# A two-layer hybrid decoder trunk on one core: the key blocks' and compressed keys' transposes and the pool branch's product stand later in TensorE's order

## The chip, the core and the metric

The kernel runs on one core of a Trainium2 chip. The core has five engines, each with its own instruction stream that it works off in order: TensorE (PE in the profile, its weight loads PEld) for matrix products, VectorE (DVE), ScalarE (ACT), GpSimd (POOL) and SyncE (SP), which here only issues DMAs. An instruction that has to wait for another engine waits at the head of its own stream, and all that is behind it waits too. The metric is the device time of one execution in microseconds (us), lower is better. It is given as the median of several runs.

## What is computed

The reference is a trunk of two layers on 512 tokens of width 1024, in float32:

```python
def _hybrid_layer(x, c, ...):
    mod = (jax.nn.silu(c) @ ada_w + ada_b).reshape(B, N_MOD, D_MODEL)
    x = x + 0.5 * g1 * _swiglu(_modulate(_rms_norm(x, norm_ffn1), sh1, sc1), ffn1_w_in, ffn1_w_out)
    h = _modulate(_rms_norm(x, norm_mix), sh2, sc2)
    u_pool, u_q, u_kv, u_gate, u_s5 = jnp.split(h @ w_in, IN_OFFSETS, axis=-1)
    y_pool = _rms_norm(_pool_mixer(u_pool, pool_w, pool_b, pool_scale), n_pool)
    y_nsa = _rms_norm(_nsa_mixer(u_q, u_kv, u_gate, ...), n_nsa)
    y_s5 = _rms_norm(_s5_mixer(u_s5, ...), n_s5)
    x = x + g2 * (jnp.concatenate([y_pool, y_nsa, y_s5], axis=-1) @ w_out)
    x = x + 0.5 * g3 * _swiglu(_modulate(_rms_norm(x, norm_ffn2), sh3, sc3), ffn2_w_in, ffn2_w_out)
    return x
```

The change lies in the middle step, the mixer. Three branches read the same projected input. The pool branch takes differences of windowed means and multiplies them by a small matrix per group. The NSA branch is attention with 8 query heads on 2 key heads: it needs keys and values of the tokens (normalised, rotated), keys and values compressed over 32 tokens by a small network, and the queries. The S5 branch is a linear recurrence.

## The kernel before

Every large product is made of three matrix products of 128x128 blocks whose operands are split into a high and a low part (`mm3`); the parts are made by ACT (high) and DVE or POOL (low). TensorE's work is the bulk of the time; DVE, ACT and POOL evacuate PSUM, normalise, split and scan.

**What sets the order.** The kernel is written as Python generators (one per chain of work), and a small planner (`Sched`, lines 337 to 378) steps them at build time. Each operation adds a cost to its engine's planned time, and a generator that says `yield t` is resumed when the planned time has come to `t`. An instruction enters its engine's stream when its generator is resumed. So `yield t + 1500.0` means: what comes next in this chain is put into the stream 1500 planned ns later than its inputs are planned to be ready, and other chains' instructions go ahead of it. The planned times set nothing but the order of the streams; on the chip each instruction waits for its own inputs. The planner's costs on TensorE are 233 ns for a matmul of 512 columns with split operands, 117 ns for 256 columns, 110 ns for a transpose, 222 ns for an unsplit one of up to 128 columns.

**PSUM and temporaries.** There are 8 PSUM banks and 9 temporary buffers of 128x512. A chain takes them at planned times (`wbank`, `bank`, `tmpn`, the last one first come, first served) and puts them back; a bank that is taken again carries a true wait on the chip for whoever read it last.

**The mixer's order on TensorE**, as the streams of both layers have it:
1. keys and values for the compression and the tokens' keys, one half of the tokens after the other (L1931 to 1966); each half ends with two blocks of keys that go through `qk_chain` with kind "k" (L1646);
2. the S5 projection (L1986 to 1994), and among its first matmuls the 16 transposes of the first half's two key blocks (L1694, four sets of four: high and low part of each block);
3. `compress(0)`, the compressed keys' first product, 16 unsplit matmuls (L1583), and among them the 16 transposes of the second half's two key blocks;
4. the pool projection, 48 matmuls (L2009); after its first nine come the S5 drive products (`s5_half`, L1751), one group for each of two halves of the channels, real parts first; three matmuls further on the compressed keys' second product (L1596);
5. `compress(1)` for the values, then their projection, 96 matmuls in four blocks (L2017); after 18 of them the two transposes of the compressed keys (L1637, 1638), after 30 more the pool branch's product of the first channel half (L1912), and after 12 more the S5 output products (L1802 to 1804), first half and second half;
6. the S5 branch's transposes and gate (L1831, L1843), the second pool product, both branches' norms (`norm_apply`), mixed with the query projection (L2270 to 2279), then attention mixed with the first half of the output projection.

**The chains that the change touches.** `qk_chain` for keys: ACT squares, DVE sums, POOL takes the power -0.5, DVE scales, POOL multiplies by gains and rotates, ACT makes the high part (L1685, 1686), DVE the low part (L1688), TensorE transposes, ACT (high) or DVE (low) evacuates (L1699). It holds two temporaries until its transposes. `compress_post` (L1591): a gelu on ACT, the second product, for the keys a norm and a rotation, then the two transposes; it holds a PSUM bank and two temporaries. `pool_chain` (L1885): sums over windows on POOL, a last step on DVE (L1909), the product, its evacuation, then the same for the second channel half, then the norm; it holds four temporaries from start to end. `s5_evac` (L1967) copies the S5 projection out of PSUM, 16 copies on ACT and 16 on DVE; `s5_chain` starts the drive products 3000 planned ns after them.

## Time and profile before

| | us |
|---|---|
| median of 3 runs | 2024.93 (2024.28 to 2029.98) |
| the profiled execution, whole time | 2025.7 |
| the profiled execution, span of the trace | 2023.9 |
| busy time of TensorE in the span | 1939.0 (96%) |
| of VectorE | 1601.9 (79%) |
| of ScalarE | 910.6 |
| of GpSimd | 530.6 |

Between the span and the whole time of the profiled execution lie 1.8 us. The page of the profile gives the busy time of each engine; the timeline gives an engine's instructions in order of time, like ones in a row merged into one row, and in square brackets how long the engine was idle before it and which engine and line ended that; the view by windows gives each engine's busy time and the granted TensorE clock (1.00 is 2.4 GHz, 0.50 is 1.2 GHz) in chosen stretches. `x4` counts instructions; an unsplit f32 matmul counts as two. Line numbers are those of helpers: L507 is every matmul, L523 every transpose, L458 every ACT operation, L467 and L471 DVE's with two and three operands, L494 POOL's.

### The profile page before, as it was taken

To read this page: it belongs to the slowest core of one execution; us is meant where nothing else is said; L and a number is where in the kernel's file an instruction comes from. 1 tells how busy PE (TensorE), PEld (TensorE's weight loads), DVE (VectorE), ACT (ScalarE), POOL (GpSimd) and SP (SyncE) were. 2 spreads that over 40 slices of the span, in tenths; PEclk is the share of its full clock that TensorE was granted. 3 is DMA by queue.
4 is the path that set the end of the run, shared out by engine and by line. 5 is a ranking of instruction groups with operands and counts; after the bars stand their busy time and mean duration, and the time that the engine had idled before them with its cause. 6 is when DMAs were issued, how large, how long until landed. Compare 5 with 4: busy or idle time off the path is not lost. (4 is left out here: it accounts for less than half of the span.)

```text
span 2023.9 us, 32544 instructions
## 1 busy us (share of the span) xinstructions
PE 1939.0 (96%) x12586; PEld 1740.2 (86%) x12586; DVE 1601.9 (79%) x2806; ACT 910.6 (45%) x1652; POOL 530.6 (26%) x755
## 2 busy tenths in 40 slices
PE   5999999998998899999999999999999989999999
PEld 3788888897887898999989899999888788898989
DVE  7789877487777788989779797788878779686866
ACT  3422222243666553534455353534437655453533
POOL 6049201744444400000020200065546360000000
PEclk9999999998998899999999999999999999999999
DMA  8668777231201125555122231413211012313222
GB/s 306 231 229 290 281 260 275 100 114 55 70 25 43 62 85 197 177 199 185 64 106 93 96 132 67 146 43 135 86 44 53 21 43 72 126 64 125 96 103 74
DMA packets 71147, 251.66 MB, mean 124 GB/s; under 512 B 8016, under 2 KB 10448, under 8 KB 70480
## 3 DMA queue, kind: packets, MB, share of 16 engines
q1 hardware_dynamic: 70992, 249.58, 35.0%
q8 instruction: 99, 1.62, 0.3%
q14 instruction: 56, 0.46, 0.1%
HBM read 247.45 MB, written 2.10 MB: 123 GB/s over the span
## 5 line engine op out<-in xcount | busy, mean ns | idle before, releaser
L507 PE MATMUL p<-s,s 128*128 128x256 f32 (+3 forms) x11926 | 1885.4, 319 | 64.9 <-DVE s L471 24.6
L507 PEld LDWEIGHTS p<-s,s 128*128 128x128 f32 x11926 | 1664.6, 191 | 249.4 <-DVE s L467 31.8
L458 ACT ACTIVATE s<-s 128x1024 fp32r<-128x1024 f32 (+6 forms) x910 | 623.1, 714 | 782.2 <-PE p L507 424.0
L467 DVE TENSOR_TENSOR s<-s,s 128x1024 fp32r<-128x1024 f32 (+9 forms) x868 | 758.5, 901 | 220.7 <-ACT s L458 214.5
L494 POOL TENSOR_TENSOR s<-s,s 128x256 f32<-128x256 f32 (+11 forms) x335 | 272.8, 833 | 251.0 <-DVE s L478 99.4
L494 POOL TENSOR_TENSOR s<-s 128x8 f32<-128x8 f32 (+4 forms) x224 | 155.2, 698 | 533.0 <-ACT s L458 362.5
L458 ACT ACTIVATE s<-p 128x512 f32<-128x512 f32 (+10 forms) x381 | 184.8, 502 | 224.7 <-PE p L507 160.3
L467 DVE TENSOR_TENSOR s<-p,s 128x512 f32<-128x512 f32 (+8 forms) x325 | 192.9, 605 | 55.0 <-ACT s L458 34.8
L471 DVE SCALAR_TENSOR_TENSOR s<-s,s 128x1024 f32<-128x1024 f32 (+3 forms) x179 | 197.9, 1110 | 8.3 <-DMA s<-in_ada_dram 7.1
L471 DVE SCALAR_TENSOR_TENSOR s<-p,s,s 128x512 f32<-128x512 f32 (+2 forms) x210 | 128.2, 619 | 55.0 <-PE p L507 50.5
L523 PE MATMUL p<-s,s 128*128 128x128 f32 (+2 forms) x532 | 82.8, 283 | 16.3 <-DVE s L467 8.3
L467 DVE TENSOR_TENSOR s<-s 128x256 f32<-128x256 f32 (+3 forms) x177 | 84.4, 491 | 12.3 <-POOL s L494 6.2
L523 PEld LDWEIGHTS p<-s,s 128*128 128x128 f32 (+2 forms) x532 | 64.8, 144 | 30.0 <-DVE s L467 8.9
L503 POOL TENSOR_SCALAR s<-s 128x128 f32<-128x128 f32 (+6 forms) x48 | 33.3, 712 | 216.7 <-PE p L507 200.5
L458 ACT ACTIVATE s<-p,s 128x512 f32<-128x512 f32 (+3 forms) x132 | 70.3, 536 | 29.6 <-DVE s L2076 19.2
L503 POOL TENSOR_SCALAR s<-s,s 128x512 f32<-128x512 f32 (+3 forms) x128 | 69.6, 562 | 31.5 <-DVE s L467 27.8
L2076 DVE CUSTOM_DVE_ANT_0 p<-p,s 128x512 f32<-128x512 f32 (+3 forms) x128 | 61.3, 498 | 7.1 <-PE p L507 6.3
L471 DVE SCALAR_TENSOR_TENSOR s<-s,s,s 128x256 fp32r<-128x256 f32 (+3 forms) x124 | 59.2, 495 | 0.6 <-ACT s L458 0.4
L458 ACT ACTIVATE s<-s,s 128x256 fp32r<-128x256 f32 x80 | 38.7, 505 | 33.3 <-DVE s L471 33.1
L471 DVE SCALAR_TENSOR_TENSOR s<-s,s,p 128x256 f32<-128x256 f32 (+1 forms) x88 | 42.3, 499 | 6.1 <-PE p L507 5.5
L467 DVE TENSOR_TENSOR s<-s,p 128x512 f32<-128x512 f32 (+1 forms) x35 | 20.6, 593 | 21.2 <-PE p L507 21.2
L471 DVE SCALAR_TENSOR_TENSOR s<-s 128x256 f32<-128x256 f32 (+3 forms) x72 | 31.1, 455 | 1.8 <-ACT s L458 1.1
(36 smaller groups left out, 226.5 us busy)
## 6 DMA issues: line engine op xcount, KB each, us to landing
s<-in_ws_dram SPq DMA_DIRECT2D x304, 512.0 KB, 4.2
s<-in_ada_dram SPq DMA_DIRECT2D x143, 512.0 KB, 5.5
s<-in_w_dram SPq DMA_DIRECT2D x4, 1024.0 KB, 7.4
s<-in_x_dram SPq DMA_DIRECT2D x8, 256.0 KB, 5.1
out_dram<-s SPq DMA_DIRECT2D x16, 128.0 KB, 1.7
s<-in_ws_dram SPq DMA_DIRECT2D x4, 420.0 KB, 3.0
s<-in_c_dram SPq DMA_DIRECT2D x2, 512.0 KB, 5.2
s<-in_bc_dram SPq DMA_DIRECT2D x2, 512.0 KB, 5.3
```

The lines of the kernel that those rows point to most:

```text
L458: nc.scalar.activation(o, i, func, **kw)
L467: nc.vector.tensor_tensor(o, a, b, op)
L471: nc.vector.scalar_tensor_tensor(o, a, s, b, op0=op0, op1=op1, **kw)
L494: nc.gpsimd.tensor_tensor(o, a, b, op)
L503: nc.gpsimd.tensor_scalar(o, a, s1, s2, op0=op0, op1=op1)
L507: nc.tensor.matmul(o, l, r, start=start, stop=stop, **kw)
L523: nc.tensor.transpose(o, i, idn)
L2076: nc.vector.tensor_tensor_reduce(b[:, :L], b[:, :L], mask, -0.125, 3.0e38, OP.add, OP.min, nmax[:, r:r + 1])
```

## The change

Three waits in planned time are made longer; no operation is added or taken away.

```diff
-CMP_SLACK = 5000.0
+CMP_SLACK = 9000.0
+KEY_SLACK = 5500.0
+POOL_SLACK = 4000.0
...
                 for a_ in range(2):
                     t = tt(lv[:, :, a_, :], xn, f(qv[:, :, a_, :]), OP.subtract)
                 tmps.put(tn, t)
-                yield t + 1500.0
+                yield t + KEY_SLACK
                 for i, src in enumerate((qq, q2)):
...
                 tt(po[:, 0:16], po[:, 0:16], v[:, 0:16], OP.subtract)
-                yield calm(stt(po[:, 16:], cur[:, 16:], rw[:, i:i + 1], v[:, 16:], OP.mult, OP.subtract))
+                yield stt(po[:, 16:], cur[:, 16:], rw[:, i:i + 1], v[:, 16:], OP.mult, OP.subtract) + POOL_SLACK
                 yield mp_ev
                 bn, b = yield from wbank()
                 yield mm(b, poolw[:, i, :], po)
```

`calm(t)` is `t + 450`. The key blocks' transposes are put 4000 planned ns later, in both halves of the tokens. `CMP_SLACK` stands twice in `compress_post` (L1594 and L1634): the second product of the compression is put 4000 ns later for keys and values, and the compressed keys' transposes 4000 ns more. The pool branch's product is put 3550 ns later, once in each channel half. All of it happens in both layers.

## Rows read from the trace of the kernel before

**Rows 1.** The page, busy time and share of each engine over the span:
```profile
PE 1939.0 (96%) x12586; PEld 1740.2 (86%) x12586; DVE 1601.9 (79%) x2806; ACT 910.6 (45%) x1652; POOL 530.6 (26%) x755
```
**Rows 2.** Timeline of TensorE, first layer (start, length, ... [idle before <- releaser]):
```profile
424.51 17.10 PE L507 MATMUL p<-s,s 128*128 128x256 f32 x141
441.45 0.60 PE L523 MATMUL p<-s,s 128*128 128x128 f32 x4
441.80 0.48 PE L507 MATMUL p<-s,s 128*128 128x512 f32 x1
...
453.79 1.00 PE L507 MATMUL p<-s 128*128 128x64 f32 x8
458.16 1.11 PE L523 MATMUL p<-s,s 128*128 128x128 f32 x4 [3.36 <-ACT s L458]
...
480.28 3.68 PE L507 MATMUL p<-s 128*128 128x64 f32 x32
...
489.27 0.27 PE L523 MATMUL p<-s,s 64*128 64x64 f32 x1 [2.93 <-DVE s L467]
```
**Rows 3.** Timeline of TensorE, second layer, the rows after the three idle times:
```profile
1443.25 1.12 PE L523 MATMUL p<-s,s 128*128 128x128 f32 x4 [3.43 <-ACT s L458]
...
1473.40 0.27 PE L523 MATMUL p<-s,s 64*128 64x64 f32 x1 [2.94 <-DVE s L467]
...
1480.74 10.45 PE L507 MATMUL p<-s,s 128*128 128x512 f32 x82 [1.80 <-DVE s L471]
```
**Rows 4.** By windows (length, busy of PE, PEld, DVE, ACT, POOL, clock, DMA, GB/s):
```profile
458.16:463.54 5.38, 5.38 (x27) 5.38 (x28) 5.00 (x18) 4.89 (x16) 0.32 (x1) 0.50 0.00 2
490.85:494.26 3.41, 3.41 (x18) 3.41 (x17) 3.41 (x6) 0.09 (x1) 0.00 (x0) 0.50 0.31 92
1443.25:1446.58 3.33, 3.33 (x17) 3.33 (x18) 3.04 (x11) 2.92 (x9) 0.32 (x1) 0.50 0.01 2
```
**Rows 5.** Timeline of POOL, first layer, gains and rotation of the second half's keys:
```profile
453.80 3.16 POOL L494 TENSOR_TENSOR s<-s,s 128x128 f32<-128x128 f32 x7 [2.87 <-DVE s L467]
```
**Rows 6.** Timeline of ACT, first layer, last row second layer:
```profile
460.08 5.57 ACT L458 ACTIVATE s<-p 32x128 f32<-32x128 f32 x18
465.67 1.28 ACT L458 ACT_TABLE_LOAD   x1
466.96 0.22 ACT L458 ACTIVATE s<-p 128x64 f32<-128x64 f32 x1
...
1445.18 5.57 ACT L458 ACTIVATE s<-p 32x128 f32<-32x128 f32 x18
```
**Rows 7.** Groups of ACT by form from 457 to 468 us (count, busy, mean ns):
```profile
L458 ACT ACTIVATE s<-p 128x512 fp32r<-128x512 f32 x2 | 1.1, 596 | 0.0
```
**Rows 8.** Timeline of DVE, first layer:
```profile
450.30 0.69 DVE L482 CAST s<-p 128x512 fp32r<-128x512 f32 x1
...
459.63 4.78 DVE L482 COPY s<-p 32x128 f32<-32x128 f32 x16
...
470.73 2.48 DVE L467 TENSOR_TENSOR s<-p,s 128x512 f32<-128x512 f32 x4 [1.79 <-PE p L507]
...
488.96 6.17 DVE L467 TENSOR_TENSOR s<-s,s 64x128 fp32r<-64x128 f32 x10
```
**Rows 9.** By windows, columns as in Rows 4, stages of both layers:
```profile
467.15:471.60 4.45, 4.45 (x37) 4.32 (x36) 1.56 (x3) 0.04 (x1) 0.10 (x1) 1.00 0.76 298
472.47:480.28 7.81, 7.81 (x35) 6.32 (x34) 7.81 (x13) 1.72 (x5) 7.73 (x12) 1.00 0.01 2
499.41:529.50 30.09, 30.09 (x224) 26.66 (x223) 17.75 (x45) 14.90 (x35) 12.20 (x20) 1.00 0.11 36
529.50:730.00 200.50, 185.41 (x1209) 164.96 (x1208) 160.48 (x403) 122.92 (x297) 85.97 (x144) 0.95 0.13 46
...
1449.08:1451.27 2.19, 2.19 (x12) 1.79 (x12) 2.11 (x4) 2.13 (x5) 0.00 (x0) 1.00 0.00 0
1513.64:1710.00 196.36, 180.43 (x1206) 160.42 (x1204) 159.79 (x403) 122.48 (x297) 86.87 (x144) 0.97 0.14 46
```

## The prediction

> **What bounds the kernel now.** The page comes first: TensorE is busy for 96% of the span [rows 1], so the change can win only the idle time that it removes, and what that idle time does to TensorE's clock. Next the timeline of TensorE through the mixer, to be read for its square brackets. The first layer has three waits there of over 1.5 us, and they stand in front of just the three things that the change moves: 3.36 before the second half's key transposes, 2.93 before the second of the compressed keys' two transposes [rows 2], and 1.81 before the pool branch's product, the idle stretch from 494.81 to 496.62 that the second layer repeats. The second layer has 3.43, 2.94 and 1.80 [rows 3]. Together 8.10 + 8.17 = 16.3 us. Then the windows behind these waits: behind the first two the granted clock is 0.50, the 1.2 GHz level, for 5.38 and 3.41 us of busy TensorE in the first layer, for 3.33 in the second, where the stretch behind the second wait is again 3.41 [rows 4]. At that level work takes twice its time, so half is lost: 2.69 + 1.71 + 1.67 + 1.71 = 7.8 us. Behind the third wait the clock is 1.00 (from 499.41 on, in [rows 9]). All that the three moves could give is 16.3 + 7.8 = 24.1 us. The question is what TensorE meets when it no longer stops there.
>
> **Where the moved instructions land.** No operation is added, so TensorE's own work is the same; what changes is what it waits for. I place the moves with the planner's costs, as an order and not as times. The second half's key sets were due 0.8 planned us into `compress(0)`, that is after 4 of its 16 matmuls, which is where the trace has the first set [rows 2]. With 4.0 more they fall 1.2 behind its 3.55, into the pool projection after five matmuls of 0.233, still ahead of the S5 drive products. The first half's sets move back within the S5 projection. The compressed keys' transposes go back by 4.0 twice and by what DVE's scans then delay their chain, and so behind both S5 output groups. The pool product goes 3.55 back, behind the first S5 output group. The S5 chain has no new slack. So with all three waits gone TensorE comes to the S5 drive products, and later to the S5 output products, earlier than now, and these are the next things that can be late.
>
> **The first move, at the S5 drive products.** TensorE would leave `compress(0)` at 453.8 + 3.5 = 457.3 (16 matmuls as the later `compress(1)` takes them, 480.28 to 483.77), then nine pool matmuls at 0.234 (7.81 us for 33 and a little else [rows 9]), 2.1, and four transpose sets at 0.35 (441.45 to 441.80), 1.4: it comes to the drive products at 460.8 [rows 2]. The key sets themselves should find their data: the first is reached at about 458.5, and what ended the wait now came at 458.16. But the drive products read the copies of `s5_evac`, and these stand in ACT's and DVE's streams behind the key splits that POOL makes late. ACT's row of 18 is 16 copies and two key evacuations of 0.60 [rows 6, 7]; it ends at 465.7, so the copies end at 464.5, DVE's at 464.4 [rows 8]. That doesn't depend on TensorE. One thing moves it: the first half's two low-part evacuations, DVE casts of 0.69 (one at 450.30, one like it at 451.79), now stand ahead of the second half's scaling for which POOL waits 2.87 [rows 5, 8]. They go behind it, wholly or in part: 0 to 1.4 us; I take 1.1, since by the planner's costs one of them lands between the two blocks' scalings. Copies done at 463.4, so 2.6 us of waiting.
>
> Then a bank. The four key sets take PSUM banks just before the drive products do, and by the planner's times the second half's drive products get banks that a key set has just put back. On the chip its evacuation by ACT stands behind the copies and, new in this order, behind the gelu with its table load: 1.28 + 0.22 + 0.60 = 2.1 [rows 6, 7]. So the second group starts at 465.5, against 467.15 + 0.9 = 468.0 now (first group at the start of that window, each group four unsplit matmuls [rows 9]). That is 2.5 gained of the 6.05 (3.36 + 2.69) lost now. In the second layer the copies end 4.4 after 1445.18 [rows 6], so at 1449.6, less 1.1, plus 2.1: 1450.6 against 1451.27 + 0.9 = 1452.2 [rows 9]: 1.6. Bounds for the bank: no wait (a bank of the copies, +1.2 each) and a second evacuation, 0.6 later.
>
> The Trainium skill, "ScalarE: Activation LUTs", section "What ACT_TABLE_LOAD costs", says that a switch of the function set costs about 1.28 us of load and 1.38 more of drain. The row agrees on the load but shows no drain: the next instruction starts at 466.96, as the load ends [rows 6]. By the page the bank would come 1.4 later in each layer, and the kernel would be 2.8 slower than I say.
>
> **The second and third move, at the S5 output products.** DVE works without a break from 470.73, where the drive products release it, to the end of the ten operations at 495.1 [rows 8]; the first half's last input is the ninth, 0.6 earlier, at 494.5. That is 26.5 us behind the second drive group's start (468.0), or 26.4 since the compressed keys' low part leaves this run. TensorE's own way from there: 18.1 to the end of the first 18 value matmuls (the second wait starts at 489.27 - 2.93 = 486.34 [rows 2], less a transpose of 0.25), some 50 more value matmuls at 0.121 (17.10 for 141 [rows 2]), 6.05, and two products of the output group that need nothing late, 0.45: 24.6. So TensorE arrives 1.8 too early and waits there. Now it loses 2.93 + 1.81 + 1.71 = 6.45 on this way; gain 4.65 in each layer. The pool product then finds DVE's last step done, one operation behind the output's inputs.
>
> **What else.** Clock: the new idle time at the drive products, 2.6 and 1.2 with 0.9 of work between, is like the waits that are followed by half clock now, and I charge 1.0 per layer (half of some 2 us; 0 to 2.7, the first layer's present loss). The wait of 1.8 is like the pool product's, which is not followed by it: 0, at most 1.7. DMA: the only transfer that the moves touch is the 1 MB load for `compress(1)`, issued when `compress(0)` has ended, which is earlier now; SP holds nothing back. Temporaries: the pool branch holds four of the nine about 9 planned us longer, and its norm, some 4 us of DVE work, moves from the query projection's first part, where DVE is busy for 17.75 of 30.09 [rows 9], towards the first attention scores; I charge 1.0 per layer, between 0 and the whole 4. Attention: 200.5 in the first layer, 196.4 in the second for the same work, with clock 0.95 and 0.97 [rows 9]; where the clock falls in it may shift by these 4 us either way, charged 0.
>
> **The sum.** First layer 2.5 + 4.65 - 1.0 - 1.0 = 5.15, second 1.6 + 4.65 - 1.0 - 1.0 = 4.25: 9.4 us. The profiled execution took 2025.7 (span 2023.9 and 1.8 around it), so 2016.3; it stood 0.8 above the median of 2024.93, and on the median I predict 2015.5.
>
> **Rivals.** *Clean*: nothing takes the waits' place, 24.1 less: 2001. For it speaks that each wait is moved past just such an engine's work; against it the copies' end at 464.5, which no move brings to 460.8. *Given back*: POOL's chain does not get earlier and half clock follows both new waits. Then the second drive group starts at 466.6 and 1451.7: gains 1.4 and 0.5, plus 2 x 4.65, less 2 x (2.7 + 1.7), less 2.0: 0.4, so 2024.5. For it speaks that DVE has no idle time from 470.73 on, against it the 1.81 that left the clock alone. *Slower*: the pool branch holds its temporaries so long that the query chains (two each) queue for them, and attention starts up to 9 us later in each layer, with TensorE idle when the projections run out: 18 less 11.4 gained, 2032. It turns to a loss of over 6 us from a slide of about 8.8 per layer. Against it: by the planner's counts only the third and fourth query chain would wait, by 2 us, and attention starts on the first.
>
> **How the numbers follow.** A measurement of this kernel can tell 0.3%, 6 us, from no change: 2018.9 to 2031.0. Forecast 0.62 (2010 to 2020, of which 0.02 lies above 2018.9), clean 0.08, given back 0.22, slower 0.08. Faster 0.60 + 0.08, same 0.02 + 0.22, slower 0.08. The range: at the good end no bank wait (2.4), no clock loss (2.0), no price for the pool branch (2.0), the rest of the casts (0.6): 16.4 gained, 2008. At the bad end "given back": 2025.
>
> **What would show it.** The three waits gone from TensorE's timeline. In their place idle time of 3 to 4.5 us at the drive products, released by ACT's or DVE's copies and then by ACT, and 1 to 2.5 before the S5 output products, released by DVE; a stretch of 0.50 clock behind the first. ACT's copies done about 1 us earlier, with the table load ahead of two evacuations. From the start of the query projection on, the old picture some 5 us earlier per layer. I am wrong if TensorE waits again at a moved transpose, if no wait appears at the S5 products, or if attention grows by more than 4 us.

## The result and the profile after

The changed kernel took 2002.37 us (median of 4, 2000.92 to 2003.53) where the kernel before took 2027.45 on the same chip; the ratio is 0.9867, with a 95% interval of 0.9828 to 0.9905. A second series gave 0.9864 (0.9839 to 0.9888). So the change gains about 24 to 27 us, and the prediction, 2015.5 with a range of 2008 to 2025, was wrong: it forecast a gain, but of 9.4 us, and the measured time lies below its range. The profiled execution took 2002.04 with a span of 2000.3, against 2023.9 before: 23.6 us less.

TensorE's share has not moved; its busy time has shrunk by 15.6 us although it does the same 12586 instructions (compare [rows 1]). The page's first part:

```profile
PE 1923.4 (96%) x12586; PEld 1723.7 (86%) x12586; DVE 1599.4 (80%) x2806; ACT 906.6 (45%) x1652; POOL 554.0 (28%) x755
```

Fewer microseconds for the same instructions go with a higher clock here: its mean over the span is 0.992 where it was 0.984. What TensorE lost at the 1.2 GHz level, half of its busy time there, fell from 29.2 to 13.9 us, which is 15.3 of the 15.6. Where that happened is seen when both traces are cut at the same instructions of TensorE's list: start of the front, first product of the second query part, end of attention, and the same again in layer 2. Columns: length, busy time and count of TensorE, its weight loads, VectorE, ScalarE, GpSimd, granted clock, DMA share, GB/s. The kernel before:

```profile
441.22:529.50 88.28, 80.17 (x513) 70.49 (x512) 67.56 (x141) 35.41 (x86) 41.07 (x61) 0.94 0.17 57
529.50:728.92 199.42, 184.33 (x1201) 163.88 (x1199) 159.47 (x402) 121.84 (x296) 85.97 (x144) 0.95 0.13 46
728.92:1426.25 697.33, 688.23 (x4984) 645.01 (x4985) 583.55 (x898) 322.86 (x507) 99.96 (x148) 1.00 0.36 126
1426.25:1513.64 87.39, 79.22 (x514) 69.55 (x512) 67.61 (x141) 35.42 (x86) 41.12 (x61) 0.96 0.17 59
1513.64:1709.08 195.44, 179.51 (x1202) 159.50 (x1199) 158.94 (x402) 121.56 (x296) 86.87 (x144) 0.97 0.14 47
1709.08:2023.90 314.82, 310.97 (x2222) 290.81 (x2222) 222.78 (x281) 133.16 (x195) 0.00 (x0) 0.99 0.29 98
```

The changed kernel, same cuts:

```profile
443.14:526.08 82.94, 77.79 (x513) 67.61 (x512) 64.41 (x138) 34.36 (x85) 46.24 (x61) 0.98 0.18 62
526.08:718.18 192.10, 178.28 (x1201) 158.26 (x1199) 161.47 (x405) 121.04 (x297) 92.97 (x143) 0.98 0.14 48
718.18:1412.38 694.20, 685.01 (x4984) 642.11 (x4985) 582.57 (x898) 322.52 (x507) 100.06 (x148) 1.00 0.36 127
1412.38:1495.32 82.94, 77.77 (x514) 67.63 (x512) 64.45 (x138) 34.37 (x85) 46.26 (x61) 0.98 0.18 62
1495.32:1687.39 192.07, 178.20 (x1200) 158.10 (x1199) 161.41 (x405) 121.02 (x297) 92.99 (x143) 0.98 0.14 48
1687.39:2000.30 312.91, 309.44 (x2222) 289.19 (x2222) 222.59 (x281) 133.00 (x195) 0.00 (x0) 1.00 0.29 98
```

Read down the first number of each row. The two fronts, where the moved steps lie, are 5.34 and 4.45 shorter: 9.8 us. The two attention stages, whose due times the change leaves alone, are 7.32 and 3.37 shorter: 10.7. The feed-forward stages give 3.13 and 1.91. The start, up to 443.14, is 1.92 longer. 9.8 + 10.7 + 5.0 - 1.9 = 23.6. A second trace of each kernel (below) gives by the means 12.3 for the fronts, 10.7 for attention, 3.8 for the feed-forward stages and 1.4 lost at the start: the part of attention stands, the others move by up to 2.5 us with the execution. The busy column of the rows at 728.92 and 1709.08 shows what kind of gain that is: in the first of them the same 4984 products take 3.2 us less, since 0.50 clock, which fell there twice in this trace of before, does not fall there in this trace of the changed kernel.

In the front, TensorE's timeline of the changed kernel (start, length, operation, shape, count, [idle before <- releaser]), layer 1 and then layer 2. Two lines were added to the program, so L509 is now every matmul and L525 every transpose:

```profile
449.86 0.60 PE L525 MATMUL p<-s,s 128*128 128x128 f32 x4
452.50 0.66 PE L525 MATMUL p<-s,s 128*128 128x128 f32 x4 [2.04 <-DVE s L469]
452.91 6.70 PE L509 MATMUL p<-s,s 128*128 128x512 f32 x21
459.44 3.68 PE L509 MATMUL p<-s 128*128 128x64 f32 x32
462.93 1.65 PE L509 MATMUL p<-s,s 128*128 128x512 f32 x6
464.43 0.60 PE L525 MATMUL p<-s,s 128*128 128x128 f32 x4
...
467.15 2.65 PE L509 MATMUL p<-s,s 128*128 128x128 f32 x19
...
494.48 2.82 PE L509 MATMUL p<-s,s 128*128 128x128 f32 x23 [1.45 <-DVE s L469]
497.23 0.33 PE L525 MATMUL p<-s,s 64*128 64x64 f32 x2
499.07 4.13 PE L509 MATMUL p<-s,s 128*128 128x512 f32 x29 [1.51 <-DVE s L473]
```

```profile
1421.75 0.66 PE L525 MATMUL p<-s,s 128*128 128x128 f32 x4 [2.05 <-DVE s L469]
...
1463.69 2.82 PE L509 MATMUL p<-s,s 128*128 128x128 f32 x23 [1.45 <-DVE s L469]
...
1468.29 1.88 PE L509 MATMUL p<-s,s 128*128 128x512 f32 x9 [1.51 <-DVE s L473]
```

Of the three waits of [rows 2, 3] the first two are gone, and the pool product, in its new place, still waits: 1.51 for 1.81 us. Two new ones have come: 2.04 in front of the last set of the key half that comes first, and 1.45 in front of the S5 output products. These waits together: 5.0 for 8.1 us per layer.

### The profile page after: what moved, and what is told of

It is laid out like the page before. It is cut to its first block, busy times and chain, and to the rows that moved or that the text cites. A ratio compares the mean times of both kernels' runs of the same rounds, so it can differ in the third digit from the quotient of the medians.

```text
span 2000.3 us, 32595 instructions
## 1 busy us (share of the span) xinstructions
PE 1923.4 (96%) x12586; PEld 1723.7 (86%) x12586; DVE 1599.4 (80%) x2806; ACT 906.6 (45%) x1652; POOL 554.0 (28%) x755
## 5 line engine op out<-in xcount | busy, mean ns | idle before, releaser
L509 PE MATMUL p<-s,s 128*128 128x256 f32 (+3 forms) x11926 | 1876.8, 318 | 68.3 <-DVE s L469 27.8
L509 PEld LDWEIGHTS p<-s,s 128*128 128x128 f32 x11926 | 1650.8, 190 | 254.6 <-DVE s L469 30.0
L460 ACT ACTIVATE s<-s 128x1024 fp32r<-128x1024 f32 (+7 forms) x910 | 621.7, 714 | 805.7 <-PE p L509 451.7
L469 DVE TENSOR_TENSOR s<-s,s 128x1024 fp32r<-128x1024 f32 (+10 forms) x868 | 766.7, 909 | 218.3 <-ACT s L460 209.4
L496 POOL TENSOR_TENSOR s<-s,s 128x256 f32<-128x256 f32 (+12 forms) x335 | 287.6, 876 | 215.0 <-DVE s L480 91.5
L496 POOL TENSOR_TENSOR s<-s 128x8 f32<-128x8 f32 (+4 forms) x224 | 159.4, 717 | 534.3 <-ACT s L460 364.5
L473 DVE SCALAR_TENSOR_TENSOR s<-s,s 128x1024 f32<-128x1024 f32 (+3 forms) x179 | 197.4, 1107 | 6.7 <-DMA s<-in_ada_dram 5.5
L473 DVE SCALAR_TENSOR_TENSOR s<-p,s,s 128x512 f32<-128x512 f32 (+2 forms) x210 | 128.0, 618 | 51.3 <-PE p L509 49.5
L469 DVE TENSOR_TENSOR s<-s 128x256 f32<-128x256 f32 (+2 forms) x177 | 84.7, 492 | 13.7 <-POOL s L496 6.2
L525 PE MATMUL p<-s,s 128*128 128x128 f32 (+2 forms) x532 | 78.7, 273 | 5.3 <-DVE s L469 5.0
L525 PEld LDWEIGHTS p<-s,s 128*128 128x128 f32 (+2 forms) x532 | 63.3, 138 | 18.1 <-DVE s L469 6.0
L460 ACT ACTIVATE s<-p,s 128x512 f32<-128x512 f32 (+3 forms) x132 | 69.3, 535 | 20.1 <-DVE s L2078 13.1
L2078 DVE CUSTOM_DVE_ANT_0 p<-p,s 128x384 f32<-128x384 f32 (+3 forms) x128 | 60.7, 504 | 4.8 <-PE p L509 3.4
L473 DVE SCALAR_TENSOR_TENSOR s<-s,s,s 128x256 fp32r<-128x256 f32 (+3 forms) x124 | 57.3, 478 | 0.6 <-ACT s L460 0.4
L473 DVE SCALAR_TENSOR_TENSOR s<-s,s,p 128x256 f32<-128x256 f32 (+1 forms) x88 | 42.3, 497 | 2.8 <-PE p L509 2.2
L473 DVE SCALAR_TENSOR_TENSOR s<-s 128x256 f32<-128x256 f32 (+3 forms) x72 | 31.0, 455 | 1.4 <-ACT s L460 1.2
```

Source lines behind the costliest of these rows:

```text
L460: nc.scalar.activation(o, i, func, **kw)
L469: nc.vector.tensor_tensor(o, a, b, op)
L473: nc.vector.scalar_tensor_tensor(o, a, s, b, op0=op0, op1=op1, **kw)
L496: nc.gpsimd.tensor_tensor(o, a, b, op)
L509: nc.tensor.matmul(o, l, r, start=start, stop=stop, **kw)
L525: nc.tensor.transpose(o, i, idn)
```

## The experiments

Below, the **front** is the stretch from 441.22 (or its like) to the first product of the second query part, **attention** the stretch from there to the end of the attention stage. **Half clock** is what it cost: half of the time in which TensorE was busy while the granted clock was 0.50, added up from the clock record of a trace. Ratios are to the kernel before on the same chip; the lengths and the half clock are of one trace each. All runs that leave TensorE's work as it is:

| run | KEY / CMP / POOL / attention due times, planned ns | ratio (95%) | fronts, us | attention, us | half clock in both attentions, us |
|---|---|---|---|---|---|
| before | 1500 / 5000 / 450 / 600 | 1 | 88.3, 87.4 | 199.4, 195.4 | 13.1 |
| before_again | the same | 0.9997 (0.9979 to 1.0016) | 90.2, 89.1 | 197.5, 197.3 | 12.1 |
| key_only | 5500 / 5000 / 450 / 600 | 0.9980 (0.9964 to 0.9995) | 88.4, 88.1 | 195.4, 198.7 | 15.0 |
| cmp_only | 1500 / 9000 / 450 / 600 | 1.0059 (1.0044 to 1.0074) | 92.2, 92.0 | 204.1, 198.1 | 21.6 |
| pool_only | 1500 / 5000 / 4000 / 600 | 0.9926 (0.9908 to 0.9943) | 86.1, 86.3 | 195.0, 195.4 | 15.8 |
| no_key | 1500 / 9000 / 4000 / 600 | 0.9936 (0.9911 to 0.9960) | 87.5, 86.4 | 196.4, 196.5 | 18.9 |
| no_cmp | 5500 / 5000 / 4000 / 600 | 0.9936 (0.9911 to 0.9961) | 78.4, 78.4 | 199.7, 201.8 | 20.1 |
| no_pool | 5500 / 9000 / 450 / 600 | 0.9980 (0.9961 to 0.9999) | 90.8, 89.1 | 195.3, 194.0 | 9.7 |
| after | 5500 / 9000 / 4000 / 600 | 0.9867 (0.9828 to 0.9905) | 82.9, 82.9 | 192.1, 192.1 | 5.7 |
| after_again | the same | 0.9864 (0.9839 to 0.9888) | 81.5, 83.0 | 192.1, 192.0 | 5.7 |
| before_att700 | 1500 / 5000 / 450 / 700 | 0.9959 (0.9939 to 0.9978) | 87.4, 87.3 | 193.8, 195.3 | 12.3 |
| before_att500 | 1500 / 5000 / 450 / 500 | 1.0009 (0.9990 to 1.0028) | 88.7, 87.3 | 195.5, 199.9 | 24.7 |
| after_att700 | 5500 / 9000 / 4000 / 700 | 0.9928 (0.9909 to 0.9948) | 82.9, 83.0 | 198.8, 198.9 | 17.8 |
| after_att500 | 5500 / 9000 / 4000 / 500 | 1.0009 (0.9994 to 1.0024) | 81.5, 82.9 | 206.7, 205.9 | 23.4 |
| pool6 | 5500 / 9000 / 6000 / 600 | 0.9916 (0.9895 to 0.9936) | 79.5, 79.5 | 201.6, 198.8 | 22.3 |
| pool6_att700 | 5500 / 9000 / 6000 / 700 | 1.0014 (1.0002 to 1.0027) | 79.5, 78.0 | 209.2, 209.2 | 38.1 |
| key_split | 5500 (second half of the tokens only) / 9000 / 4000 / 600 | 0.9963 (0.9945 to 0.9981) | 83.5, 84.9 | 198.7, 196.5 | 16.7 |

The front's end stands up to 10 products (some 1.3 us) earlier or later in TensorE's list from row to row, with the same number (2472) in before, cmp_only, after, both repeats and the four runs with 500 or 700 on the fronts of before and after.

### The same program again, and each edit alone

```diff
-KEY_SLACK = 1500.0     key_only: 5500
-CMP_SLACK = 5000.0     cmp_only: 9000
-POOL_SLACK = 450.0     pool_only: 4000
```

> The program of the kernel before, unchanged, profiled once more: it tells how much of a trace belongs to the program and how much to the one execution. Theory F (the front: the gain of the change lies in the mixer's front, where the instructions were moved, and the rest of the trace differs because the clock fell at other places): the waits of TensorE stand where they stood, at most 0.1 us apart (3.4, 2.9 and 1.8 us in each layer's front), but the stretches at half clock in the attention stages and the feed-forward stages stand elsewhere and their number changes by 4 or more of 16; the ratio to before is 1.000. Theory O (the order: what the scheduler makes of the attention stages after the change is what shortened them): the stretches at half clock stand behind the same waits again, 14 or more of 16 at the same instructions, since the program decides them; the ratio is 1.000 as well.

> The due time of the key blocks' transposes alone (5500 for 1500). Theory F: of each layer's three waits the first (3.4 us) and its two stretches at half clock go, a wait of 2.0 us in front of the fourth set of the first half comes, as in the changed kernel, and the waits of 2.9 and 1.8 us stay: front shorter by 1 to 3 us a layer, the whole 2018 to 2024 us. The attention stages are ordered differently from both kernels, and by F their length keeps to 195 to 200 us. Theory O: the attention stages take 190 to 193 us each, as after the whole change (190.6 and 191.1 against 199.4 and 195.4), and the whole is 2008 to 2014 us.

> The due time of the compressed keys' steps alone (9000 for 5000); TensorE's order in both attention stages is that of the kernel before, instruction by instruction. Theory F: the wait of 2.9 us and the stretch at half clock behind it go in each layer, and a part of it comes back at the S5 output products, which still need VectorE's chain: 0.5 to 3 us shorter a layer, the whole 2019 to 2026 us. Theory O: since the attention order is the old one, nothing is won there, and the whole stays at 2022 to 2027 us; the two attention stages stay within 3 us of 199.4 and 195.4.

> The due time of the pool branch's product alone (4000 for 450). Its product moves behind 9 products of the first query part in each layer, and the attention order changes (388 lines of TensorE's list). Theory F: the wait of 1.8 us goes and nothing takes its place: 1.5 to 2 us a layer and 1 to 2 more from the clock, the whole 2019 to 2023 us. Theory O: the attention stages lose 4 to 9 us in layer 1 and 3 to 5 in layer 2, and the whole is 2008 to 2016 us.

**The same program** put half clock at other places and paid 25.4 us for it over the whole span, against 29.2; so single stretches belong to the execution, as theory F had it. One wait differed: the third of layer 1 was 3.34 us instead of 1.81. This is where it stood, and its like in the two transposes' edits alone; the rows are TensorE's timeline of before_again, key_only and cmp_only:

```profile
489.67 0.27 PE L525 MATMUL p<-s,s 64*128 64x64 f32 x1 [2.94 <-DVE s L469]
...
497.01 3.56 PE L509 MATMUL p<-s,s 128*128 128x512 f32 x14 [3.34 <-DVE s L473]
```

```profile
488.12 0.27 PE L525 MATMUL p<-s,s 64*128 64x64 f32 x1 [1.30 <-DVE s L469]
488.33 0.63 PE L509 MATMUL p<-s,s 128*128 128x256 f32 x3
495.44 4.91 PE L509 MATMUL p<-s,s 128*128 128x512 f32 x15 [6.49 <-DVE s L473]
```

```profile
500.29 9.43 PE L509 MATMUL p<-s,s 128*128 128x512 f32 x61 [7.87 <-DVE s L473]
```

The row released by `DVE s L473` is the pool branch's product. In before_again half clock did not follow the 2.94 wait, TensorE took 1.5 us less from there to the pool product, and waited 1.5 longer for it. Counted from the start of layer 1's front, TensorE came to the pool product after 53.6 us in before, 47.5 in key_only and 49.7 in cmp_only; the product started after 55.4, 54.0 and 57.6. So key_only came 6.1 us sooner, of which 1.4 were left there, and half clock behind it (2.6 us) took the rest. cmp_only came 3.9 us sooner and started it 2.2 later, since VectorE's step came later. So the waits do not add up: TensorE takes its list in order, the time of the pool product was set by VectorE, and what is won ahead of it piles up in front of it. Theory F's gains of 0.5 to 3 us a layer for key_only and cmp_only did not come, and cmp_only's 2042 us lie outside theory O's 2022 to 2027 too. pool_only came out where theory O had it (2013.99 us), but theory O's ground, shorter attention stages, holds for 3.4 and 1.0 us of it against the mean of the two traces of before, while the fronts gave 3.1 and 1.9.

### Each edit left out

> The compressed keys' and the pool product's due times, without that of the key blocks' transposes. Theory P (pile-up: the pool branch's product, which TensorE reaches in order and which needs VectorE's step at 494.6 to 495.7, holds whatever the other two edits save; with it out of the way they pay): the 3.4 us wait with its half clock stays, the 2.9 us wait goes, the pool product's wait is under 2 us: 5 to 9 us less than the pool product's edit alone cannot come, 0 to 5 can: 2009 to 2014 us. Theory O (the attention order alone pays, and it came with the pool product's edit): as the pool product's edit alone, 2012 to 2016 us, with the front's saving lost again somewhere.

> The key blocks' and the pool product's due times, without that of the compressed keys. Theory P: the 3.4 us wait and its two stretches at half clock go, a 2.0 us wait comes earlier, the compressed keys' wait stays at 1 to 3 us, the pool product's wait is under 2 us: 4 to 10 us less than the pool product's edit alone, 2003 to 2010 us. Theory O: 2012 to 2016 us.

> Both transposes' due times, without that of the pool branch's product. Theory P: TensorE comes to the pool product some 6 us before VectorE's step and waits 6 to 9 us in each layer, with half clock behind it: 2022 to 2042 us, no faster than before. Theory F (each wait that is removed pays for itself, as the prediction's sum had it): the 1.8 us wait of before grows by at most 2 us: 2012 to 2018 us.

> The changed kernel once more, on the chip of these runs, where the kernel before took 2032 us (median of 19) rather than 2025 to 2027. If the gain belongs to the programs, the ratio is 0.983 to 0.990 and the half clock costs 12 to 17 us of the span against 25 to 29 in the kernel before; if half of it was this one execution's luck with the clock, the ratio is 0.990 to 0.995 and the half clock costs 20 us or more.

The pile-up (theory P) shows in no_pool: both transposes moved, the pool product not.

```profile
497.08 3.33 PE L509 MATMUL p<-s,s 128*128 128x512 f32 x8 [8.93 <-DVE s L473]
```

The fronts take 90.8 and 89.1: two of the three edits gain nothing there. With the pool product moved as well (no_cmp) the key blocks' move pays at once: fronts 78.4 for 86.1 and 86.3. But the whole of no_cmp, 2016 us, is no better than pool_only, 2014, and far from the 2003 to 2010 that theory P gave: its attention stages take 199.7 and 201.8 with 20.1 us of half clock. The third edit, added to these two, makes the fronts longer (82.9) and yet the kernel 14 us faster, with 8 to 10 us less in each attention stage. No theory of the front explains that. no_key, 2016 us, lies above theory P's 2009 to 2014 as well; its pool product still waits 2.61 us in both layers where theory P gave under 2. The repeated changed kernel shows that it is no accident of one execution: 0.9864, and the attention stages 192.1 and 192.0 again.

### Only the attention order

```diff
-ATT_SLACK = 600.0
+ATT_SLACK = 700.0      (or 500.0)
```

This due time stands in the attention steps alone. The fronts keep their order instruction by instruction; some 250 to 290 lines of TensorE's list within the attention stages stand otherwise.

> The kernel before with nothing but the due times of the attention steps set from 600 to 700: the fronts keep their order instruction by instruction, and 280 lines of TensorE's list inside the attention stages stand otherwise. Theory L (the attention stage is a draw: any reshuffling moves its half clock by several us, and the changed kernel drew well): the half clock costs of the two attention stages differ from before's (9.3 and 3.8 us, 6.8 and 5.4 in the second trace) by more than 3 us in one direction or the other, and the whole by 4 to 15 us. Theory C (the attention stage got quieter because the front was moved, whatever its order): the whole is 2026 to 2033 us with half clock as in before.

> The changed kernel with nothing but the due times of the attention steps set from 600 to 700: same fronts, 264 lines of TensorE's list inside the attention stages otherwise. Theory L: the attention stages lose their low half-clock cost (2.9 us each in two traces) and come to 5 to 10 us each: 2006 to 2018 us. Theory C: they keep 2 to 4 us each: 1999 to 2005 us.

> The changed kernel with the due times of the attention steps set from 600 to 500: same fronts, 248 lines of TensorE's list inside the attention stages otherwise. Theory L (the attention order is a draw, and the changed kernel's was a good one): the fronts keep 82.9 us each, the attention stages pay 5 to 10 us of half clock each and the whole is 2006 to 2018 us. Theory C (the moved front makes quiet attention stages likely): half clock 2 to 4 us each, 1999 to 2005 us.

> The kernel before with the due times of the attention steps set from 600 to 500: same fronts, 288 lines of TensorE's list inside the attention stages otherwise. Theory L (the order is a draw on either front): fronts of 87 to 90 us each, half clock in the attention stages anywhere from 3 to 14 us each, the whole 2012 to 2040 us, and by more than 3 us off the kernel before. Theory C (the moved front is what makes quiet attention stages possible): 2022 to 2035 us, attention stages with 5 us or more of half clock each.

With the changed front the three orders gave 0.9867, 0.9928 and 1.0009: the whole gain of the change is lost again by a due time of 500 instead of 600 in steps that the change doesn't touch. The fronts stayed (81.5 to 83.0). The attention stage of after_att700, beside the row at 526.08 above, same instructions, same idle time (13.7 us for 13.8), 6.7 us longer at clock 0.95:

```profile
524.60:723.40 198.80, 185.05 (x1201) 163.45 (x1199) 160.88 (x405) 121.48 (x297) 91.76 (x143) 0.95 0.14 46
```

Theory C, 1999 to 2005 us for both, fails; theory L (a draw) has the kind of thing right, but not its size: after_att500, at 11.7 us of half clock a stage and 2029 us, lies beyond its 5 to 10 and 2018. With the front of before, three orders gave 1, 0.9959 and 1.0009. There before_att500 had 11.6 us more half clock in attention than before and 8.4 us less idle time, and so came within 1.3 us of it, where theory L wanted more than 3; theory C's numbers fit that run. The mean of three orders is 0.9989 there and 0.9935 on the changed front: 0.0054, or 11 us, between the 9.8 and 12.3 that the fronts differ by. That is the best guess at what the change itself is worth, and no more than that, since the three draws on the changed front lie 0.0142 apart; the rest is that 600 happened to go with a quiet order.

The order alone does not fix the price either. cmp_only and before_fill (below) have the attention order of before instruction by instruction on TensorE, and their traces show 21.6 us of half clock there each, where the two traces of before show 13.1 and 12.1.

### Filling the waits

> The kernel before with TensorE kept at work in two of each layer's front waits: 13 idle products 128x512 into the bank of the key set that waits 3.4 us, 11 into the bank of the compressed keys' transposes that wait 2.9 us; the transposes then overwrite them, nothing else of any engine's order is changed, and the idle products are no part of the computation. Theory H (it is the half clock behind the waits that costs, beside the waits themselves): the transposes start when they started, the stretches at half clock behind them go, and each front is 3 to 4 us shorter (lost 4.4 and 3.4 us in the one trace, 4.8 and 5.1 in the other): 2017 to 2024 us on a chip where the kernel before takes 2030, ratio 0.995 to 0.998. Rival R (half clock falls as often wherever TensorE idled in the microseconds around, or by chance, and the filler is itself late work): the front keeps its length or grows by up to 1 us a layer, ratio 0.999 to 1.001.

> The changed kernel with TensorE kept at work in the two waits of each layer that half clock followed in its trace: 8 idle products 128x512 in the 2.0 us wait of the first half's last key set, 26 of 128x256 ahead of the first feed-forward product behind the attention stage (waits of 0.95, 2.5 and 1.0 us). They are no part of the computation. Theory H: up to 1.7 us a layer at the first place (half clock followed it in 3 of 4 stages) and 2.9 to 3.4 at the second (4 of 4), less up to 1 us that the filler overruns: 1993 to 1998 us, ratio 0.995 to 0.998 of the changed kernel. Rival R: 2000 to 2005 us.

> The changed kernel with 26 idle products 128x256 ahead of the first feed-forward product behind each attention stage (they are no part of the computation), and nothing else: every other instruction stands where it stood. In the changed kernel waits of 0.95, 2.5 and 1.0 us stand there with 6.8 us at half clock behind them in 4 of 4 stages. Theory H: half clock there goes or halves, and each layer ends 1.7 to 3.4 us earlier: 1995 to 1999 us, ratio to the changed kernel 0.996 to 0.998. Rival R (half clock falls elsewhere instead, behind the next wait, or the stage's end is set by VectorE): 2000 to 2005 us.

```diff
                     bk, bb = yield from wbank()
+                    if blkno == 2 and i == 0:
+                        for _ in range(13):
+                            nc.tensor.matmul(bb, st["h"][0][:, 0, 0:128], st["h"][0][:, 0], start=True, stop=True)
```

before_fill (13 here, 11 at the compressed keys' transposes), TensorE, layer 1:

```profile
455.63 3.23 PE L1699 MATMUL p<-s 128*128 128x512 f32 x13
459.21 0.66 PE L525 MATMUL p<-s,s 128*128 128x128 f32 x4 [0.35 <-ACT s L460]
...
485.92 2.68 PE L1640 MATMUL p<-s 128*128 128x512 f32 x11
488.54 0.27 PE L525 MATMUL p<-s,s 64*128 64x64 f32 x1
489.26 0.27 PE L525 MATMUL p<-s,s 64*128 64x64 f32 x1 [0.45 <-DVE s L469]
...
496.61 5.58 PE L509 MATMUL p<-s,s 128*128 128x512 f32 x26 [3.34 <-DVE s L473]
```

In layer 1 the filler did what it should: the key set starts as its data come, 16.95 us behind the front's start as before, and the front's half clock fell from 4.4 to 1.7 us. But the pool product started only 1.0 us sooner (54.4 us behind the front's start for 55.4): its wait grew from 1.81 to 3.34, and the 1.7 us of half clock now follow it. The front took 88.7 us for 88.3. In layer 2 the halves of the tokens come in the other order, so the block that the edit names comes first, and the 13 products stand at the front's very start, more than 10 us ahead of the wait. There they are work done early: the wait shrinks to 0.52, the front's half clock is 2.8 for 3.4, and the front takes 89.9 us for 87.4. The kernel is not faster: 1.0016 (0.9998 to 1.0034), near the rival's 0.999 to 1.001, though not for its reason. So theory H was tested in one layer, and there its gain came and was lost at the pool product. The tail's filler in after_tail took away one of the two stretches at half clock behind the wait of 2.5 us in both layers, but a wait of 1.38 us remained behind the filler, and each attention stage became only 0.6 us shorter (191.5 and 191.4): ratio 0.9868 (0.9854 to 0.9883), as the changed kernel, 2001.5 us for the 1995 to 1999 of theory H. after_fill, with a filler at the 2.0 us wait besides, was no better: 0.9881 (0.9853 to 0.9909). In its layer 2 these products stand behind the drive products, for the same reason, and are 1.9 us of added work. In layer 1 they told what that wait is:

```profile
451.19 2.10 PE L1700 MATMUL p<-s 128*128 128x512 f32 x8 [2.04 <-DVE s L469]
```

The idle products read nothing that is late, and waited 2.04 us as well, for the bank they write. So the changed kernel's new wait is for a PSUM bank that VectorE empties, not for the keys. No filled kernel beats the changed one.

### The two remaining waits of the changed front

```diff
-                yield t + KEY_SLACK
+                yield t + (KEY_SLACK if blkno > 1 else 1500.0)      key_split
-POOL_SLACK = 4000.0
+POOL_SLACK = 6000.0                                                 pool6; pool6_att700 with ATT_SLACK 700
```

> The changed kernel with the due time 5500 for the second half's key transposes alone, the first half's at 1500 as before. The 2.0 us wait of the first half's last set, which waits for its bank, goes in each layer; TensorE comes to the S5 drive products some 2 us earlier and waits there for the copies of the inputs up to 2.6 us (the wait that the prediction set there and that the changed kernel doesn't show). If it does, the prediction's third step was right in kind and the 2.0 us wait stood in its place: front 82 to 84 us, no gain. If not, the front is 79 to 81 us. The attention order is a new draw: 1998 to 2015 us for the whole.

> The changed kernel with the pool product's due time 6000 for 4000: it moves behind more products of the first query part. By the front alone: the 1.5 us wait for VectorE's step goes in each layer, at most 3 us in all, 1997 to 2002 us. By theory L this is a new draw of the attention order, and what it pays in half clock there (2.9 us a stage in the changed kernel) decides: 3 to 10 us a stage, 2000 to 2015 us.

> The changed kernel with the pool product at 6000 and the attention steps at 700: the front of the run with 6000 (79.5 us to the first product of the second query part, with 10 products fewer before it), 136 lines of TensorE's list in the attention stages otherwise than there. Theory L: half clock of 3 to 13 us a stage: 1996 us with a draw as good as the changed kernel's, 2015 us with one as bad as that run's; a quiet one comes in the smaller part of the draws. Theory C: 1996 to 2003 us.

key_split takes the 2.0 us wait out of layer 1, and there the wait comes that the prediction had set at the S5 drive products:

```profile
461.59 0.95 PE L509 MATMUL p<-s,s 128*128 128x512 f32 x3
465.44 4.54 PE L509 MATMUL p<-s,s 128*128 128x128 f32 x19 [2.90 <-ACT s L460]
```

In layer 2, where the halves come in the other order, the same edit leaves the late due time to the half that comes first. The 2.04 us wait stayed there, and nothing waits at the drive products:

```profile
1430.65 0.66 PE L525 MATMUL p<-s,s 128*128 128x128 f32 x4 [2.04 <-DVE s L469]
```

One or the other, within one kernel. The whole, 2020 us, lies above the 1998 to 2015 expected. pool6 has 0.58 left of the 1.51 us wait and the shortest front of a kernel with all three edits, 79.5 (with 10 products fewer in it); with attention at 600 and 700 it took 2011 and 2031 us. The second has 38.1 us of half clock in its attention stages, 19 a stage, where theory L gave 3 to 13 and no more than 2015 us.

## Why the prediction was wrong, step by step

**The bound.** Reading the three waits as what the change could win was right for the front and too narrow for the kernel. The ceiling of 24.1 us counted 16.3 + 7.8 in the front alone; what came was 9.8 there and 13.8 elsewhere. The "clean" rival has the measured time, 2001, for reasons that did not occur: two new waits and a shorter third took the old ones' place. That its number came out is luck.

**Where things land.** Predicted after five pool matmuls, the second half's key sets stand after six. The compressed keys' transposes stand behind both S5 output groups, as said; the pool product, set behind the first of them, stands behind both too.

**The drive products.** TensorE was to come at 460.8 and wait 2.6 for the copies, then 1.2 for a bank. It came at 467.15 and waited for nothing. The step failed in place, not in size: the first half's last key set waited 2.04 for its bank, half clock followed for 3.38 us (1.7 lost), and this execution was 1.9 later from the start: 460.8 + 2.0 + 1.7 + 1.9 = 466.4; the other 0.7 are 12 pool products and three key sets ahead of it, 4.2 us, for the nine and four that I put at 3.5. So one of the prediction's own signs of being wrong came: TensorE waits at a moved transpose. The window of the changed kernel behind that wait (columns as above, clock third from the end):

```profile
453.62:457.00 3.38, 3.38 (x10) 2.60 (x9) 2.93 (x5) 0.12 (x1) 3.22 (x8) 0.50 0.29 105
```

The 3.7 us stand for the 3.8 and 1.0 that I charged; that they come near is luck, for it is another wait. key_split shows the copies' wait, 2.90 for 2.6, released by ScalarE as said. That a moved transpose also takes another bank I saw for the second half only. The bank wait behind the gelu shows nowhere: by 467.15 the table load was over. ScalarE's timeline:

```profile
460.63 4.44 ACT L460 ACTIVATE s<-p 32x128 f32<-32x128 f32 x16
465.09 1.28 ACT L460 ACT_TABLE_LOAD   x1
466.39 0.71 ACT L460 ACTIVATE s<-p 128x64 f32<-128x64 f32 x2
```

The copies end at 465.09, where they ended at 464.5 before (the row of 18 in [rows 6] less two evacuations); against this execution's start, 1.9 later, that is 1.3 earlier, for 1.1 predicted, and the two evacuations stand behind the load as said. The Trainium skill's "ScalarE: Activation LUTs", section "What ACT_TABLE_LOAD costs", adds about 1.38 us of drain to the load. The trace shows none here either: the load starts 0.02 us after the copies end and the next instruction 0.02 after the load's 1.28, and the 2.8 us estimated by that page did not come.

**The S5 output products.** Wait predicted 1.8, measured 1.45 in both layers. TensorE arrives 25.0 us after the second drive group's start (468.05 to 493.03; 24.6 predicted), VectorE's chain is done after 26.4 (26.4 predicted). The wait is right; that the chain's length came out is luck, for it is no longer the chain of [rows 8], which ran without a break. VectorE's row of before, then two of the changed kernel's with one of GpSimd (POOL) between them:

```profile
479.16 9.88 DVE L1774 TENSOR_TENSOR_SCAN s<-s,s 128x128 f32<-128x128 f32 x12
```

```profile
482.83 1.35 DVE L1776 TENSOR_TENSOR_SCAN s<-s,s 128x128 f32<-128x128 f32 x4
483.04 5.71 POOL L496 TENSOR_TENSOR s<-s,s 64x8 f32<-64x8 f32 x3 [0.91 <-DVE s L473]
492.20 5.39 DVE L469 TENSOR_TENSOR s<-s,s 128x508 f32<-128x508 f32 x4 [1.18 <-POOL s L496]
```

The 16 scans take 12.8 us before and 8.7 after: 0.39 us each where GpSimd does no large operation beside them, mostly 1.2 to 1.75 where it does. On its side a GpSimd operation of 64x8, which took 0.31 us before, takes 5.37 beside the short scans, as far as the profile tells GpSimd's times. VectorE then stands still for 1.06 and 1.18 us, and its last 128x508 operations, 0.67 us each before, take up to 1.74 beside GpSimd's. So the 26.4 is what two engines left each other, and not a fixed length.

That the pool product then finds its data was wrong: 1.51 us each. I charged 1.0 a layer for the pool branch, for another reason.

**Half clock in the front.** Charged 1.0 a layer; 1.7 in three of the four fronts of the changed kernel's two traces, 0 in the fourth.

**The sum for the front.** 9.4 predicted, or 11.4 without the 1.0 a layer for what the pool branch would do behind it; 9.8 measured, 12.3 by the means of two traces each. The size is right, two of its terms by luck, as said.

**What failed** is the last line of "What else": attention charged 0, with 4 us either way. Half clock there fell from 13.1 to 5.7 us and idle time from 31.0 to 27.7, and half clock in the feed-forward stages from 4.9 to 0 (1.7 in the second trace of before, so that most of this belongs to the execution). I took the attention stages for the same work in the same order, shifted. They are not: the planner lays out everything behind a moved step anew, and the edits change some 400 lines of TensorE's list there. [rows 9] had the clue, clocks of 0.95 and 0.97 for the same stage in two layers. The draw is worth far more than 4 us: with nothing but other attention orders the changed front gave ratios of 0.9867 to 1.0009, some 28 us apart. A forecast that knew this would have had about 2012 in its middle, 0.9935 of 2024.93 by the mean of the three orders, and a range of some 15 us to either side.

**Open** is what makes an attention stage quiet. The idle time of the stage does not tell: before_att500 idled for 11.4 and 11.2 us and paid 9.4 and 15.4 of half clock, the changed kernel idled for 13.8 and paid 2.9 a stage. Nor does the busy share of one stretch. Windows of one part of the attention stage, pool6_att700 and then the changed kernel (columns as above):

```profile
627.30:634.20 6.90, 6.90 (x23) 4.99 (x23) 2.70 (x6) 1.97 (x5) 0.00 (x0) 0.51 0.02 8
634.20:644.40 10.20, 8.79 (x63) 7.54 (x63) 7.45 (x27) 7.32 (x24) 2.43 (x6) 1.00 0.00 0
644.40:661.50 17.10, 15.80 (x62) 13.66 (x62) 9.39 (x35) 7.23 (x25) 8.59 (x17) 0.50 0.34 124
```

```profile
606.00:616.00 10.00, 8.97 (x64) 8.10 (x63) 9.55 (x45) 8.87 (x33) 5.69 (x10) 1.00 0.00 2
616.00:623.00 7.00, 5.98 (x38) 4.66 (x37) 6.57 (x17) 5.48 (x12) 7.00 (x14) 1.00 0.01 2
623.00:630.00 7.00, 6.13 (x38) 4.68 (x37) 6.15 (x20) 4.29 (x15) 2.22 (x3) 1.00 0.21 75
630.00:640.00 10.00, 9.76 (x68) 8.39 (x69) 8.30 (x34) 8.52 (x28) 6.13 (x14) 1.00 0.01 2
```

Ahead of 17.1 us at 1.2 GHz TensorE was busy for 86% of 10.2 us; in the changed kernel it was busy for 85 to 90% through 24 us, and stayed at 2.4 GHz. The two are not alike in what came before: in pool6_att700 the clock had been at 0.51 until 634.2. Whether the changed front makes quiet orders likelier is open too: of the six orders on it or near it one paid under 6 us, the others 16.7 to 38.1; of the three on the front of before none paid under 12.

## What to carry to other kernels

Where a scheduler lays out the work, an edit's gain is its own part plus a new draw for all that stands behind it. Cut both traces at the same instructions and look at where the time went before crediting the edit; then change a due time that has nothing to do with it, and see how far that alone moves the kernel. And in an in-order list waits don't add: of three waits the last one decides, and removing the earlier ones first (key_only, cmp_only, no_pool) gains at most 0.2% or loses.

## What the hardware showed unexpectedly

TensorE's half clock cost 10.9 to 48.7 us of some 2000 in the table's kernels, and it weighed in most comparisons. It followed waits, but not by their length alone: over the table's traces from 400 us on, the waits of 2.3 to 2.6 us, nearly all at the end of attention with two of about 1 us beside them, had it around them or in the next 5 us in all 37 cases, those of 2.9 to 3.0 in 8 of 11, those of 3.3 to 3.5 in 15 of 16, the waits of 1.85 us in the feed-forward stage in 8 of 32. The same program puts it behind the 2.93 us wait of [rows 2] in one execution and not in the next, and the identical attention order of before, before_again and before_fill paid 9.3, 6.8 and 14.0 us for it in layer 1. Time bought back from the clock ahead of a step that another engine sets was lost again at that step in before_again and before_fill. It was kept in after_again: there no half clock followed the 2.05 us wait of layer 1, ahead of the drive products that start VectorE's chain, and the whole front was 1.5 us shorter (81.5 for 82.9).

VectorE's scans took 0.39 us or up to 1.75 for the same 128x128, by what GpSimd did beside them; an engine's chain read off one trace is therefore no fixed length when the order of another engine changes.
